# Low halves of the down projections' weights: an adding DMA onto negated high halves in place of a VectorE subtraction

## The chip, the cores and the metric

The kernel runs on one core of a Trainium2 chip. The metric is device time in microseconds, from the first to the last instruction of one execution and the little that lies around them, median over the executions. The engines have short names here: PE is the tensor engine, DVE the vector engine, ACT the scalar engine, POOL is GpSimd, SP the sync engine, which in this kernel issues nearly all transfers. A name with a q behind it (SPq) is an engine's queue of instructions that are not compute.

## The reference

One decoder layer on 256 positions with 2048 channels, all in float32: a half-step SwiGLU feed-forward (hidden size 5632), a mixer of a state-space group and a gated MLP group, a second feed-forward, and a gated embedding. Only the feed-forwards matter for the change:

```python
def swiglu(x, w_gate, w_up, w_down):
    return (jax.nn.silu(x @ w_gate) * (x @ w_up)) @ w_down
...
    h = h + 0.5 * swiglu(rms_norm(h, norm_ffn1[i]), w1_gate[i], w1_up[i], w1_down[i])
...
    h = h + 0.5 * swiglu(rms_norm(h, norm_ffn2[i]), w2_gate[i], w2_up[i], w2_down[i])
```

## The kernel before

**Three products for one.** Every large product is done in the tensor engine's rounded float32 format, with both operands split in two: a high half (the value rounded to that format) and a low half (the value less its high half). For each weight `w` there are `wh` and `wl`, for each activation a high and a low one, and `products` issues three matmuls for each tile: activation high by `wh`, activation high by `wl`, activation low by `wh`. They add up in one PSUM accumulator (`acc`).

**Units.** A Group is a product with 512 output columns (`n0`), over `kt` tiles of 128 rows of the weight. A load takes four of these tiles (128 x 2048 float32, 1 MB) into one of three `raw` buffers. A pair (`KS = 2` tiles, half a load) is the unit of the splitting and of the products: its `wh` and `wl` are tiles of 128 x 1024, each from a pool of four buffers, and it feeds 12 matmuls (2 tiles x 2 halves of the positions x 3). The down projections are `w1_down` and `w2_down`: 4 groups of 44 tiles each, so 22 pairs in a group and 88 pairs in each of the two.

**Order.** The kernel's order is written out by hand in `stream`. For pair i on PE it first calls `do_split` up to pair i + 3, then issues the products of pair i. `do_split` issues loads two ahead on SP, then ACT's copy of `raw` to `wh` (line 133), then DVE's subtraction `wl = raw - wh` (line 134). Since `wh` and `wl` have four buffers, the split of pair i + 3 can begin when the products of pair i - 1 are done, and is needed when the products of pair i + 2 are done. A load's buffer comes free when ACT and DVE have read it. At the end of a down group `down_post` adds the accumulators to `h` (DVE, line 390), squares (ACT, line 223), and transposes `h` on PE, with splits on ACT and DVE (lines 214 and 217).

In the down projections the activations are `gTa` and `gTb`, so the matmuls of these stages can be told by their names `gTah`, `gTal`, `gTbh`, `gTbl`. GpSimd has no DMA of its own in this kernel.

Of the kernel before, what the change touches and what calls it, by code (L numbers as in the profile page):

```python
# [7 lines left out]
F32 = mybir.dt.float32  # L8
F32R = mybir.dt.float32r
I32 = mybir.dt.int32  # L10
AF = mybir.ActivationFunctionType
ALU = mybir.AluOpType
# [9 lines left out]
NW = 512  # L22
KL = 4
# [25 lines left out]
class Group:  # L49
    def __init__(self, w, n0, kt, act, post, kbase=0):  # L50
        self.w, self.n0, self.kt, self.act, self.post, self.kbase = w, n0, kt, act, post, kbase
        self.ps = None


class Layer:
# [9 lines left out]
        self.queue.append([self.tick_no + delay, gen])  # L65

    def paced(self, gen):
        """emits what gen emits, at most about self.budget us of VectorE time in a tick; gen yields
        the time of what it emitted (a float) or the ticks to wait (an int)"""
        acc = 0.0  # L70
        for c in gen:
            if isinstance(c, int):
                yield c
                acc = 0.0
            else:
                acc += c
                if acc >= self.budget:
                    yield 1
                    acc = 0.0
# [14 lines left out]
    def stream(self):  # L94
        nc = self.nc
        subs, loads = [], []
        for g, k0, nk in self.plan:
            li = len(loads)
            loads.append((g, k0, nk))
            for s0 in range(0, nk, KS):  # L100
                subs.append((g, li, s0, k0 + s0, min(KS, nk - s0)))
        n = len(subs)
        tail = self.plan[-1][0]
        n_tail = sum(sb[0] is tail for sb in subs)
        raws, split = {}, {}
        state = {"ld": 0, "sp": 0}

        def load(li):
            for f in self.preload.pop(li, ()):
                f()  # L110
            g, k0, nk = loads[li]
            t = self.raw_p.tile([P, KL, NW], F32, tag="raw", name="raw")
            kq, kr = divmod(g.kbase + k0, KL)
            nc.sync.dma_start(out=t[:, 0:nk, :], in_=g.w[g.n0 // NW, kq, :, kr:kr + nk, :])
            raws[li] = t

        def do_split():
            i = state["sp"]
            state["sp"] += 1
            g, li, s0, k0, nk = subs[i]  # L120
            while state["ld"] <= min(li + 2, len(loads) - 1):
                load(state["ld"])
                state["ld"] += 1
            for f in self.presplit.pop(i, ()):
                f()
            src = raws[li][:, s0:s0 + nk, :]
            if g is tail and i < n - LA_SPLIT - 1:
                wh = self.pools["tail"].tile([P, KS, NW], F32R, tag=f"wh{i}", name="wht")
                wl = self.pools["tail"].tile([P, KS, NW], F32R, tag=f"wl{i}", name="wlt")
            else:  # L130
                wh = self.wh_p.tile([P, KS, NW], F32R, tag="wh", name="wh")
                wl = self.wl_p.tile([P, KS, NW], F32R, tag="wl", name="wl")
            nc.scalar.activation(out=wh[:, 0:nk, :], in_=src, func=AF.Copy)  # L133
            nc.vector.tensor_tensor(  # L134
                out=wl[:, 0:nk, :], in0=src, in1=wh[:, 0:nk, :].bitcast(F32), op=ALU.subtract)
            split[i] = (wh, wl)

        def products(i, ts, ps=None, c0=0, c1=NW):
            g, li, s0, k0, nk = subs[i]
            wh, wl = split[i]  # L140
            for j in range(nk):
                k = k0 + j
                for t in ts:
                    ah, al = g.act(k, t)
                    first, last = k == 0, k == g.kt - 1
                    o = (ps or g.ps[t])[:, c0:c1]
                    nc.tensor.matmul(o, ah, wh[:, j, c0:c1], start=first, stop=False)  # L147
                    nc.tensor.matmul(o, ah, wl[:, j, c0:c1], start=False, stop=False)  # L148
                    nc.tensor.matmul(o, al, wh[:, j, c0:c1], start=False, stop=last)  # L149

        for i in range(n):
            ahead = i + LA_SPLIT + 1
            if i > n - 2 * n_tail:
                ahead += (i - (n - 2 * n_tail)) // 2
            while state["sp"] < min(ahead, n):
                do_split()
            g, li, s0, k0, nk = subs[i]
            if k0 == 0:
                g.ps = [self.acc_p.tile([P, NW], F32, tag="acc", name=f"acc{t}") for t in range(2)]
            if g is tail:  # L160
                products(i, (0,))
            else:
                products(i, range(2))
                split.pop(i)
            if k0 + nk == g.kt:
                self.spawn(g.post(g, 0, 0) if g is tail else g.post(g))
            self.tick_no += 1
            self.run_due()
        late = self.acc_p.tile([P, NW], F32, tag="acc", name="late")
        for part, ps in enumerate((tail.ps[1], late)):  # L170
            for i in range(n - n_tail, n):
                products(i, (1,), ps, part * NW // 2, (part + 1) * NW // 2)
                self.tick_no += 1
                if i == n - 1:
                    tail.ps[1] = ps
                    self.spawn(tail.post(tail, 1, part))
                self.run_due()
        while self.queue:
            self.tick_no += 1
            self.run_due()  # L180
# [28 lines left out]
            out=dl, in0=src, scalar=g, in1=dh.bitcast(F32), op0=ALU.mult, op1=ALU.subtract)  # L209

    def split_gain2(self, ps, g, dh, dl):
        """two k tiles that lie in one bank; g, dh, dl start at the first of them"""
        for kk in range(2):
            self.nc.scalar.activation(out=dh[:, kk, :], in_=ps[:, kk * 256:kk * 256 + 256], func=AF.Copy,
                                      scale=g[:, kk:kk + 1])
        for kk in range(2):
            self.nc.vector.scalar_tensor_tensor(
                out=dl[:, kk, :], in0=ps[:, kk * 256:kk * 256 + 256], scalar=g[:, kk:kk + 1],
                in1=dh[:, kk, :].bitcast(F32), op0=ALU.mult, op1=ALU.subtract)
# [3 lines left out]
        self.nc.scalar.activation(out=j, in_=src, func=AF.Square, accum_out=acc)  # L223

    def h_to_T(self, n, gcol):
        """transposes of chunk n of h, gain applied, into hT"""
        for b in range(2):
            yield 1
            k0 = 4 * n + 2 * b
            ps = self.transposes(  # L230
                [self.h[:, t, (k0 + kk) * P:(k0 + kk + 1) * P] for kk in range(2) for t in range(2)])
            self.split_gain2(ps, self.gcol[:, gcol + k0:gcol + k0 + 2], self.hTh[:, k0:k0 + 2], self.hTl[:, k0:k0 + 2])
# [4 lines left out]
    def kernel(self):  # L237
        tc, nc, I = self.tc, self.nc, self.i
# [27 lines left out]
        self.ffn_groups(2)  # L266
        self.ple_groups()

        # products that nothing reads keep the tensor engine's clock up until the first weights are here
        warm = self.aux_p.tile([P, NW], F32, tag="aux", name="warm")  # L270
        for _ in range(N_WARM):
            nc.tensor.matmul(warm[:, 0:P], self.ident, self.ident, start=True, stop=True)
# [48 lines left out]
        self.pools.pop(key)  # L321
        self.cms.pop(key).__exit__(None, None, None)

# [1 line left out]
    KA = 24  # L325

    def open_g(self):
# [15 lines left out]
    def ffn_groups(self, which):  # L343
        I = self.i
        wg, wu, wd = (I[f"w{which}_{n}"] for n in ("gate", "up", "down"))
# [59 lines left out]
                self.whole(gate)  # L405
            self.whole(Group(wu, c * NW, 16, self.act_hT, up_post(c)))
        for n in range(4):
            self.whole(Group(wd, n * NW, 44, act_g, down_post(n)))

# [1 line left out]
    def vexp(self, pool, x, out):  # L411
        """out = exp(x) for [128, 32] tiles, relative error of a few 2^-24"""
        v = self.nc.vector
        t = {n: pool.tile([P, 32], F32, tag=f"ex{n}", name=f"ex{n}") for n in "xnra"}
        v.tensor_scalar(out=t["x"], in0=x, scalar1=-88.0, scalar2=88.5, op0=ALU.max, op1=ALU.min)
# [15 lines left out]
    def s5_tables(self):  # L431
        nc, I, g, v = self.nc, self.i, self.nc.gpsimd, self.nc.vector
# [25 lines left out]
        are, aim, ldt = (prm[:, i, :] for i in range(3))  # L458
# [74 lines left out]
        for k in range(NQ):  # L533
# [6 lines left out]
            u1, u2, bbr, bbi = (T(n, (P, 8, 16)) for n in ("u1", "u2", "bbr", "bbi"))  # L540

            def cmul(xr_, xi_, yr, yi, outs_r, outs_i, neg=False):
                """(xr_ + i xi_)(yr + i yi); the imaginary part negated on demand"""
                gop(u1, yr, xr_, M)
                gop(u2, yi, xi_, M)
                yield 0.4
# [18 lines left out]
            for i in range(2):  # L565
                s = slice(64 * i, 64 * i + 64)
# [20 lines left out]
            for q in range(8):  # L587
                o = ps[64 * (q % 2):64 * (q % 2) + 64, 32 * (q // 2):32 * (q // 2) + 32]
                for ri in range(2):
                    nc.tensor.matmul(o, ea[ri][:, q].rearrange("p t g x -> p (t g x)"),  # L590
                                     cp[ri][:, q].rearrange("p g x -> p (g x)"),
                                     start=(ri == 0), stop=(ri == 1))
# [4 lines left out]
            for a in range(2):  # L597
                s = slice(64 * a, 64 * a + 64)
# [22 lines left out]
                    yield cost  # L621
            put(k, 0, 2, 512)

# [1 line left out]
    def close_mix(self):  # L625
        for n in ("yss", "mix", "qt"):
            self.close(n)
# [29 lines left out]
        self.nc.sync.dma_start(out=self.qt[b], in_=self.stash[b])  # L657

    def s5_block(self, n):
        """four pairs of groups: 2 * 64 states and 2 * 32 channels each"""  # L660
        nc, g, v = self.nc, self.nc.gpsimd, self.nc.vector
        m = self.pools["mix"]
        qt = self.qt[n]
# [4 lines left out]
        u = m.tile([P, 256], F32, tag=f"u{par}", name="u")  # L668
        nc.scalar.activation(out=u, in_=ps[:, 0:256], func=AF.Copy)
        yield 1  # L670
        # one bank for each half of the rows of the tensor engine
        vb = [self.aux_p.tile([P, NW], F32, tag="aux", name=f"v{x}") for x in range(2)]
        for ri in range(2):
            for i in range(4):
# [246 lines left out]
        for n in range(4):  # L921
            G(Group(wo, n * NW, 8, act_ss, wo_post(n, self.r[5], True)))

# [1 line left out]
    def ple_groups(self):  # L925
        I, nc = self.i, self.nc
        r = self.r[4]
# [165 lines left out]
```

## Time and profile before

| | |
|---|---|
| device time, median of 2 runs (lowest to highest) | 1886.81 us (1885.71 to 1887.91) |
| profiled execution, span | 1884.0 us |
| PE busy | 1868.6 us (99%) |
| DVE busy | 1118.2 us (59%) |
| ACT busy | 842.7 us (45%) |
| POOL busy | 57.5 us (3%) |
| moved by DMA | 373.64 MB, 198 GB/s on average |

The page says how long each engine was busy and what moved. The timeline gives single instructions with the idle time of their engine before them. The windows give sums for a stretch, with the granted clock (1.00 is TensorE's higher level, 2.4 GHz, and 0.50 the lower, 1.2 GHz) and the mean busy share of the 16 DMA engines.

### The profile page before, as it was taken

What the parts mean: (1) busy time and instruction counts of PE and PEld (TensorE: products, weight loads), DVE (VectorE), ACT (ScalarE), POOL (GpSimd) and SP (SyncE); (2) the same over time, 40 slices, a digit from 0 to 9 for tenths busy, and PEclk for the clock granted to TensorE, in tenths of its full rate; (3) what the DMA queues carried; (4) which work ended last, traced back from release to release, by engine and by line L of the source; (5) the groups of instructions that cost most, each with busy time, mean ns of one, the idle gap of its engine ahead of it and who ended that gap; (6) DMA issues with size and microseconds to landing.
All of it is one profiled execution on the core that took longest, in us unless ns stands there. A gap on an engine that the chain in (4) does not pass through costs nothing.

```text
span 1884.0 us, 21981 instructions
## 1 busy us (share of the span) xinstructions
PE 1868.6 (99%) x8752; PEld 1551.3 (82%) x8752; DVE 1118.2 (59%) x1516; ACT 842.7 (45%) x1014; POOL 57.5 (3%) x60
## 2 busy tenths in 40 slices
PE   9999999999999999999999999999999999999998
PEld 7888888888888888887888888888888888888887
DVE  6788886455445554688876545455544444455565
ACT  6444444444444444434446544444444444344454
POOL 1000000000000000033100000000000000000000
PEclk9999999999999999999999999999999999999999
DMA  8556665554555555665545555555555555555553
GB/s 330 197 208 237 237 228 222 182 198 178 189 193 198 182 196 182 230 240 199 189 161 179 201 181 199 180 197 182 183 197 187 193 184 196 190 190 188 198 201 134
DMA packets 62534, 373.64 MB, mean 198 GB/s; under 512 B 7776, under 2 KB 13152, under 8 KB 19808
## 3 DMA queue, kind: packets, MB, share of 16 engines
q1 hardware_dynamic: 62000, 371.67, 54.7%
q8 instruction: 68, 1.11, 0.2%
q10 hardware_dynamic: 432, 0.57, 0.1%
q14 instruction: 34, 0.28, 0.0%
HBM read 360.55 MB, written 11.53 MB: 197 GB/s over the span
## 4 chain that ended last, share of the span: by engine, by line
PE 53%; DVE 0%; POOL 0%; issue 0%; ACT 0%; POOLq 0%; DVEq 0%; ACTq 0%
PE acc L147 17%; PE acc L149 17%; PE acc L148 17%; PE tr L199 1%; PE sp L766 0%; PE y L725 0%; POOL gv L843 0%; PE v L678 0%; DVE tf L701 0%; PE y L719 0%; PE late L149 0%; PE late L148 0%; PE late L147 0%; DVE gv L841 0%; DVE tb L701 0%
## 5 line engine op out<-in xcount | busy, mean ns | idle before, releaser
L134 DVE TENSOR_TENSOR wl<-raw,wh 128x1024 fp32r<-128x1024 f32 (+1 forms) x649 | 801.9, 1237 | 661.1 <-ACT wh L133 657.8
L133 ACT ACTIVATE wh<-raw 128x1024 fp32r<-128x1024 f32 (+1 forms) x649 | 686.2, 1058 | 773.3 <-PE acc L149 745.1
L147 PE MATMUL acc<-wh,hTh 128*128 128x512 f32 (+1 forms) x1744 | 684.8, 393 | 0.2 <-ACT wh L133 0.2
L148 PE MATMUL acc<-wl,hTh 128*128 128x512 f32 (+1 forms) x1744 | 678.5, 389 | 0.8 <-DVE wl L134 0.8
L149 PE MATMUL acc<-wh,hTl 128*128 128x512 f32 (+1 forms) x1744 | 679.1, 389 | 0.0
L149 PEld LDWEIGHTS acc<-wh,hTl 128*128 128x128 f32 x1744 | 327.4, 188 | 68.6
L148 PEld LDWEIGHTS acc<-wl,hTh 128*128 128x128 f32 x1744 | 327.7, 188 | 67.9 <-DVE wl L134 1.8
L147 PEld LDWEIGHTS acc<-wh,hTh 128*128 128x128 f32 x1744 | 327.6, 188 | 66.9 <-ACT wh L133 0.6
L147 PE MATMUL acc<-wh,gTah 128*128 128x512 f32 x384 | 150.9, 393 | 0.0
L149 PE MATMUL acc<-wh,gTal 128*128 128x512 f32 x384 | 149.7, 390 | 0.0
L148 PE MATMUL acc<-wl,gTah 128*128 128x512 f32 x384 | 149.5, 389 | 0.0
L148 PE MATMUL acc<-wl,gTbh 128*128 128x512 f32 x320 | 124.5, 389 | 0.0
L149 PE MATMUL acc<-wh,gTbl 128*128 128x512 f32 x320 | 124.5, 389 | 0.0
L147 PE MATMUL acc<-wh,gTbh 128*128 128x512 f32 x320 | 124.5, 389 | 0.0
L149 PEld LDWEIGHTS acc<-wh,gTal 128*128 128x128 f32 x384 | 72.1, 188 | 15.2
L148 PEld LDWEIGHTS acc<-wl,gTah 128*128 128x128 f32 x384 | 72.2, 188 | 14.6
L147 PEld LDWEIGHTS acc<-wh,gTah 128*128 128x128 f32 x384 | 72.1, 188 | 14.5
L149 PEld LDWEIGHTS acc<-wh,gTbl 128*128 128x128 f32 x320 | 60.1, 188 | 12.5
L147 PEld LDWEIGHTS acc<-wh,gTbh 128*128 128x128 f32 x320 | 60.1, 188 | 12.5
L148 PEld LDWEIGHTS acc<-wl,gTbh 128*128 128x128 f32 x320 | 60.1, 188 | 12.4
L194 POOL TENSOR_TENSOR r<-rs,mhalf 128x2 f32<-128x2 f32 x6 | 5.1, 856 | 1354.6 <-DVE rs L193 1343.8
L360 ACT ACTIVATE g<-acc,r 128x512 f32<-128x512 f32 x44 | 29.9, 689 | 19.8 <-PE acc L149 19.8
(227 smaller groups left out, 1065.7 us busy)
## 6 DMA issues: line engine op xcount, KB each, us to landing
raw<-in_w_up SPq DMA_DIRECT2D x88, 1024.0 KB, 4.8
raw<-in_w_down SPq DMA_DIRECT2D x88, 1024.0 KB, 4.8
raw<-in_w_gate SPq DMA_DIRECT2D x86, 1024.0 KB, 4.8
raw<-in_w_in SPq DMA_DIRECT2D x24, 1024.0 KB, 4.9
raw<-in_w_out SPq DMA_DIRECT2D x16, 1024.0 KB, 4.8
raw<-in_w_ple_gate SPq DMA_DIRECT2D x16, 1024.0 KB, 4.8
qt<-stash SPq DMA_DIRECT2D x8, 1152.0 KB, 5.2
stash<-qt SPq DMA_DIRECT2D x8, 640.0 KB, 4.5
```

The source lines that it names most:

```text
L133: nc.scalar.activation(out=wh[:, 0:nk, :], in_=src, func=AF.Copy)
L134: nc.vector.tensor_tensor(out=wl[:, 0:nk, :], in0=src, in1=wh[:, 0:nk, :].bitcast(F32), op=ALU.subtract)
L147: nc.tensor.matmul(o, ah, wh[:, j, c0:c1], start=first, stop=False)
L148: nc.tensor.matmul(o, ah, wl[:, j, c0:c1], start=False, stop=False)
L149: nc.tensor.matmul(o, al, wh[:, j, c0:c1], start=False, stop=last)
L194: nc.gpsimd.tensor_tensor(out=out, in0=s2, in1=self.mhalf, op=ALU.pow)
L199: self.nc.tensor.transpose(ps[:, i * P:(i + 1) * P], b, self.ident)
L360: self.nc.scalar.activation(out=st[c][t], in_=g.ps[t], func=AF.Silu, scale=r[:, t:t + 1])
```

## The change

In the groups of the down projections, a pair with an index that `lo_dma` divides gets its `wl` in another way. ACT copies `wh` into `wl` with the sign turned, and a DMA issued by GpSimd then reads the weights of the pair from HBM once more and adds them to what stands in `wl`: `wl = -wh + w`. In the first down projection this is every second pair (44 of 88), in the second every pair (88). The other pairs, and all other products, keep the subtraction on DVE. The other hunks of the diff only take out comments.

```diff
@@ class Group
         self.ps = None
+        self.lo_dma = 0
...
@@ Layer.stream, do_split
             nc.scalar.activation(out=wh[:, 0:nk, :], in_=src, func=AF.Copy)
+            if g.lo_dma and i % g.lo_dma == 0:
+
+                nc.scalar.activation(out=wl[:, 0:nk, :], in_=wh[:, 0:nk, :].bitcast(F32), func=AF.Copy, scale=-1.0)
+                kq, kr = divmod(g.kbase + k0, KL)
+                nc.gpsimd.dma_start(out=wl[:, 0:nk, :], in_=g.w[g.n0 // NW, kq, :, kr:kr + nk, :], accum_op=ALU.add)
+                split[i] = (wh, wl)
+                return
             nc.vector.tensor_tensor(
                 out=wl[:, 0:nk, :], in0=src, in1=wh[:, 0:nk, :].bitcast(F32), op=ALU.subtract)
             split[i] = (wh, wl)
...
@@ Layer.ffn_groups
         for n in range(4):
-            self.whole(Group(wd, n * NW, 44, act_g, down_post(n)))
+            g = Group(wd, n * NW, 44, act_g, down_post(n))
+            g.lo_dma = 2 if which == 1 else 1
+            self.whole(g)
```

ACT's instructions where the first down projection begins (line 133 before and 134 after are the copy to `wh`, 203 and 211 belong to the activations); the number behind a name is that of its buffer. Before:

```order
L133 ACTIVATE wh_4060<-raw_3990 128x1024
L133 ACTIVATE wh_4076<-raw_3990 128x1024
L133 ACTIVATE wh_4094<-raw_4024 128x1024
L133 ACTIVATE wh_4112<-raw_4024 128x1024
L203 ACTIVATE gTbh_2924<-tr_4130 128x512
```

and with the change:

```order
L134 ACTIVATE wh_4060<-raw_3990 128x1024
L134 ACTIVATE wh_4076<-raw_3990 128x1024
L137 ACTIVATE wl_4077<-wh_4076 128x1024
L134 ACTIVATE wh_4095<-raw_4024 128x1024
L134 ACTIVATE wh_4113<-raw_4024 128x1024
L137 ACTIVATE wl_4114<-wh_4113 128x1024
L211 ACTIVATE gTbh_2924<-tr_4132 128x512
```

The new copy stands behind the `wh` of the second half of each load, so the added transfer of a load comes right after the point where its `raw` buffer is given back.

GpSimd's queue at the same place, with the change (616 and 617 belong to tables set up long before; 139 is the adding DMA); before, the same queue had no DMA here:

```order
L616 MEMSET qt_352 128x8
L617 MEMSET qt_352 128x8
L139 DMA wl_4077<-in_w1_down 128x1024
L139 DMA wl_4114<-in_w1_down 128x1024
L139 DMA wl_4165<-in_w1_down 128x1024
```

The second down projection on ACT, with the change:

```order
L134 ACTIVATE wh_11472<-raw_11363 128x1024
L137 ACTIVATE wl_11473<-wh_11472 128x1024
L134 ACTIVATE wh_11491<-raw_11399 128x1024
L137 ACTIVATE wl_11492<-wh_11491 128x1024
L134 ACTIVATE wh_11508<-raw_11399 128x1024
L137 ACTIVATE wl_11509<-wh_11508 128x1024
```

Here every copy to `wh` is followed by its negation, two instructions for a pair where there was one.

## Rows read from the trace of the kernel before

**Rows 1.** The page: span, and busy time, share and instructions of each engine
```profile
span 1884.0 us, 21981 instructions
PE 1868.6 (99%) x8752; PEld 1551.3 (82%) x8752; DVE 1118.2 (59%) x1516; ACT 842.7 (45%) x1014; POOL 57.5 (3%) x60
```

**Rows 2.** Waits of PE over the whole span: waiting line <- releaser: us, times, longest
```profile
PE sp L766 <- POOL gv L843: 4.4, 1, 4.4
PE warm L272 <- POOL mhalf L251: 1.4, 1, 1.4
PE acc L148 <- DVE wl L134: 0.8, 1, 0.8
PE acc L147 <- ACT wh L133: 0.2, 1, 0.2
```

**Rows 3.** Second down product, timeline: start us, us, engine line op [idle before <-releaser]
```profile
1621.11 0.39 PE L149 MATMUL acc<-wh,gTal 128*128 128x512 f32 x1
1621.34 0.39 PE L147 MATMUL acc<-wh,gTah 128*128 128x512 f32 x1
1621.54 1.06 ACT L133 ACTIVATE wh<-raw 128x1024 fp32r<-128x1024 f32 x1 [1.66 <-PE acc L149]
1621.57 0.39 PE L148 MATMUL acc<-wl,gTah 128*128 128x512 f32 x1
1622.63 1.23 DVE L134 TENSOR_TENSOR wl<-raw,wh 128x1024 fp32r<-128x1024 f32 x1 [1.49 <-ACT wh L133]
1623.88 5.77 SPq L114 DMA_DIRECT2D raw<-in_w_down  x2
1624.26 1.06 ACT L133 ACTIVATE wh<-raw 128x1024 fp32r<-128x1024 f32 x1 [1.66 <-PE acc L149]
1629.72 0.39 PE L148 MATMUL acc<-wl,gTbh 128*128 128x512 f32 x1
```

**Rows 4.** Windows (length; busy PE, PEld, DVE, ACT, POOL; clock; DMA share; GB/s): downs, start-up
```profile
560.00:614.40 54.40, 54.40 (x245) 45.03 (x244) 27.41 (x26) 23.12 (x28) 0.00 (x0) 1.00 0.53 192
1620.00:1674.40 54.40, 54.40 (x245) 45.06 (x244) 27.38 (x26) 23.16 (x28) 0.00 (x0) 1.00 0.52 191
10.00:35.00 25.00, 24.23 (x105) 19.31 (x105) 16.66 (x23) 19.04 (x35) 3.87 (x6) 1.00 1.01 406
```

**Rows 5.** DMA of 15 to 35 us: all packets, and one queue issue row
```profile
DMA packets 1601, 8.33 MB, mean 417 GB/s; under 512 B 432, under 2 KB 432, under 8 KB 688
raw<-in_w_up SPq DMA_DIRECT2D x4, 1024.0 KB, 9.1
```

**Rows 6.** The page: DMA issues, KB each, median us from issue to landing
```profile
raw<-in_w_down SPq DMA_DIRECT2D x88, 1024.0 KB, 4.8
raw<-in_w_ple_proj SPq DMA_DIRECT2D x4, 512.0 KB, 3.7
```

**Rows 7.** ACT in the timeline at the end of a second-down group
```profile
1590.64 1.06 ACT L133 ACTIVATE wh<-raw 128x1024 fp32r<-128x1024 f32 x1 [1.66 <-PE acc L149]
...
1594.98 1.04 ACT L133 ACTIVATE wh<-raw 128x1024 fp32r<-128x1024 f32 x1
...
1597.25 1.06 ACT L133 ACTIVATE wh<-raw 128x1024 fp32r<-128x1024 f32 x1
...
1600.46 1.06 ACT L133 ACTIVATE wh<-raw 128x1024 fp32r<-128x1024 f32 x1
```

**Rows 8.** Windows as in group 4: around a wait of PE, and at the start
```profile
880.00:882.00 2.00, 0.00 (x0) 0.00 (x0) 1.97 (x3) 0.14 (x1) 2.00 (x1) 0.98 0.91 385
884.00:886.00 2.00, 2.00 (x11) 2.00 (x11) 1.97 (x4) 0.00 (x0) 0.00 (x0) 0.50 0.00 0
890.00:892.00 2.00, 2.00 (x12) 1.63 (x11) 2.00 (x7) 0.00 (x0) 1.49 (x2) 1.00 0.88 340
10.00:12.00 2.00, 1.23 (x5) 0.86 (x5) 1.73 (x3) 0.91 (x3) 0.00 (x0) 1.00 0.95 322
```

**Rows 9.** By tile: durations ns min/median/max of SP's issue and of GpSimd's longest operation
```profile
L114 SPq DMA_DIRECT2D raw<-in_w_down x88: 327/328/328, 487.4 to 1751.0; - x88
L843 POOL TENSOR_TENSOR gv<-gv,gvb x2: 2396/3693/4990, 872.0 to 878.6; 128x1024 f32<-128x1024 f32 x2
```

## The prediction

> **What bounds the kernel now.** I read the page's busy times first: PE is busy 1868.6 of 1884.0 us, DVE 59%, ACT 45% [rows 1]. The list of PE's waits comes next. Four waits, 6.8 us in all, are the whole of what PE waited for during 1884 us; only one of 0.8 us is for DVE's subtraction, and none stands in a down projection [rows 2]. The windows over the two down projections say the same for the stages that are changed: PE 54.40 of 54.40 us at a granted clock of 1.00, DVE 27.4, ACT 23.1, POOL 0, and the 16 DMA engines 0.52 to 0.53 busy at 191 to 192 GB/s [rows 4]. So in these stages TensorE is the bound and everything else has room. DVE's work, which the change takes away, costs nothing there now.
>
> The timeline shows how much room. ACT begins a `wh` every 2.72 us (1621.54 and 1624.26), the period of one pair of 12 matmuls. The copy begins just after the last matmul that reads the old content of that buffer (start 1621.11, 0.39 us) has ended, takes 1.06 us, and DVE's subtraction follows at 1622.63 and takes 1.23 us, to 1623.86. The first matmul that reads this `wl` is that of three pairs later: 1621.57 + 3 x 2.72 = 1629.73, which is the row at 1629.72. So `wl` now lies finished for 5.9 us before it is wanted [rows 3].
>
> **What the change removes.** In 132 of 176 pairs DVE loses a subtraction of 1.23 us. With no wait of PE on it in these stages, the gain is 0. The most that any change off PE could bring in the whole kernel is 1884.0 - 1868.6 = 15.4 us, and that lies in waits and in the start and the tail elsewhere [rows 1, 2].
>
> **What it adds on ACT.** One copy of 128 x 1024 for each such pair. A negating copy does not occur in this trace; the nearest row is the copy to `wh`, same engine, size and function, 1.06 us [rows 3]. In the second down projection ACT then works 2 x 1.06 = 2.12 us of each 2.72, and at a group's end the squares and splits delay it: `wh` at 1594.98 is 1.7 us late against 1590.64 + 2.72, the next two 1.2 and 1.7 us [rows 7]. ACT still fits; what it costs is the start of the transfer behind it.
>
> **The new deadline.** The chain of a pair becomes copy, negation, GpSimd's issue, transfer. From ACT's start 1621.54 the negation ends at about 1621.54 + 2 x 1.06 = 1623.7. The deadline stays at 1629.7. So from the end of the negation to the landing there are L = 6.0 us. If the landing comes x later, PE stands still, and since a buffer comes back every fourth pair, it stands x once in four pairs: 22 times in each of the two stages. Behind GpSimd's waiting DMA only further adding DMAs are queued, and no other engine wants GpSimd there.
>
> **What the adding transfer costs.** There is no adding DMA and no DMA issued by GpSimd in the trace, so I bound both. From below: it costs what a plain 512 KB load costs, 3.7 us to landing [rows 6], and its issue SP's 0.33 us [rows 9]. Then L holds, and the load of the DMA engines goes from 1 MB to 2 MB for each two pairs. From above: it costs three passes over 512 KB (read the weights, read `wl`, write `wl`, each like a plain load), and GpSimd's issue takes as long as its longest operation here, 3.7 us [rows 9]. Between them I take two passes: a plain load reads 512 KB, this one reads 1 MB, the weights and the old `wl`. The nearest row is then the plain 1 MB load with 4.8 us to landing [rows 6].
>
> For what the DMA engines can carry I read the start-up, the only stretch where they are full: 417 GB/s in 15 to 35 us, at a share of 1.01 over 10 to 35 us, and 1 MB loads land after 9.1 us there [rows 4, 5]. So 1 MB (1.049 million bytes) is 2.51 us of all 16 engines. Two pairs last 2 x 2.72 = 5.44 us.
>
> Second down projection: 1 MB plain and two adding transfers of two passes are 3 MB, 3 x 2.51 = 7.54 us against 5.44 (with r passes 2.51 x (1 + r)). The DMA engines become the bound, 2.10 us late for each two pairs, 44 times: +92 us. With the share as measured in these stages in place of the rate (0.52 x 5.44 = 2.83 us for 1 MB [rows 4]) it is 8.49 us, +134 us.
>
> First down projection: one adding transfer for two pairs, 2 MB, 5.03 us of 5.44. This fits, but with little room, and the added transfer begins about when the plain load does, which SP issues when the second `wh` of its buffer is made, 1.1 us ahead of the end of the negation. Of the plain load's 2.51 us up to 1.4 can lie ahead of it: 4.8 + 1.4 = 6.2 us, and with half a microsecond for GpSimd's slower start (my choice; no row has it) 6.7, 0.7 over L. 22 x 0.7 = +15 us; by the bounds 0 (3.7 us) and 22 x 3.1 = +68 us (9.1 us). ACT's delay at the ends of the 4 groups, 1.7 us each, adds 7 us. In the second stage it hides behind the full DMA engines.
>
> There is a rule of the Trainium skill on an adding DMA, and it speaks against the change: in "Collectives: The Full Stack", section "The bandwidth ceiling: the fold count and why AG ≠ RS ≠ AR", a reduce step runs at about half a copy's rate, because it reads two sources on one read ring. By it the second stage is bound as in the sum above; with the plain 512 KB row alone there would be no such bound. No run here shows it yet.
>
> **Sum.** 0 (DVE) + 92 + 15 + 7 = +114 us. The profiled span is 1884.0 us, 2.8 below the median of the runs, 1886.8; on that median: 2001 us.
>
> **Rivals.**
>
> *Hidden.* The added read of `wl` is free beside the read from HBM: one pass. Then two pairs of the second stage need 5.03 us of 5.44 and the landing keeps L. Price 0, time 1887; with small misses up to 1915. For it: 0.47 of the DMA engines is idle in these stages [rows 4], and a 512 KB load lands in 3.7 us. Against it: 92% of what the engines ever carried would have to go without queueing. It decides at (5.44 - 2.51) / 2.51 = 1.17 passes: above that the second stage cannot hold 2.72 us. Its sign is the other one: not slower. Nothing makes the kernel faster by 2% (38 us), since only 15.4 us are idle on PE.
>
> *Late, not full.* One pass, but a long way: GpSimd's issue or the completion takes long, and each landing comes up to 9.1 us after the negation, as in the start-up. 22 x 3.1 = 68 us in each stage, +136 at most, 1930 to 2020. It would show in both stages alike, where my forecast shows almost all in the second.
>
> *Three passes, or a slow GpSimd.* Second stage: 2.51 + 2 x 3.77 = 10.06 us for two pairs, +4.62 x 44 = 203; first: 6.28, +0.84 x 44 = 37; together +240, 2127 us. A GpSimd that needs 3.7 us for one issue would bound the second stage alone: 0.98 x 88 = +86, inside my range.
>
> *The clock falls.* PE's one long wait in the trace (4.4 us) was followed by a granted clock of 0.50, the 1.2 GHz level, in 884 to 886, and it was 1.00 again by 890; a window at the start in which PE stood still for 0.77 of 2 us kept 1.00 [rows 2, 8]. My stalls are 1 to 2 us for each pair or two. If they too bring the clock down in half of the second stage, a pair there takes 5.44 instead of 3.77 us: 44 x 1.67 = +73 on top, 2074.
>
> **How the numbers follow.** Two passes with full DMA engines: 0.50, of its own range 1960 to 2075 (below: 1.8 passes, 2.51 x 2.8 = 7.03 us for two pairs, +70, and nothing in the first stage; above: the 134 us, or the clock). Hidden: 0.24. Late, not full: 0.08. Three passes and more: 0.17. Faster: 0.01. The prediction is the likeliest, 2001 us. A range that leaves out 2 in 10 reaches down to the hidden case and gives up the three passes: 1886 to 2075. By 2%, about what a measurement of this kernel can tell from no change (38 us): faster 0.01, same 0.24, slower 0.75.
>
> **What would show it.** In the windows of the second down projection: DMA share near 1.0, PE busy near 5.44 / 7.54 = 0.72, the stage about 330 us in place of 240. PE's waits should name the DMA of `wl` at the matmul on `wl`, some 90 us in the second stage, 10 to 25 in the first. The landing of the adding DMA: above 6 us in both, near 7 in the first, 8 to 10 in the second. ACT should have no wait for DVE there. The prediction is wrong if the DMA share of the second stage stays well below 1 while PE waits (then it is the way, not the load), if the first stage loses as much as the second, or if PE does not wait at all.

## The result and the profile after

The changed kernel takes 2036.29 us (median of 2 runs, 2032.15 to 2040.43) against 1886.81: a ratio of 1.079, 95% interval 1.077 to 1.081, so 149.5 us slower. The forecast was 2001 us, in a range of 1886 to 2075. The sign was right, and so was what holds the second stage, which lost the most; the loss of the first stage was put at less than half of what it was.

The page of the changed kernel, span and busy times, which answer to [rows 1]:

```profile
span 2030.5 us, 22257 instructions
PE 1906.5 (94%) x8752; PEld 1549.8 (76%) x8752; DVE 958.5 (47%) x1384; ACT 981.0 (48%) x1146; POOL 169.0 (8%) x192
```

DVE fell by 160 us and ACT rose by 138, as the change says; the span rose by 146.5. PE's "busy" rose by 38 us although its matmuls are the same 8752. PE's waits answer to [rows 2] (us in total, times, longest):

```profile
PE acc L156 <- DMA wl<-in_w_down: 107.7, 84, 3.0
PE sp L776 <- POOL gv L853: 4.4, 1, 4.4
PE acc L156 <- DVE wl L142: 1.4, 2, 0.8
```

One line is new: PE waits 107.7 us for the DMA into `wl`, in 84 waits. By stage, the first down projection and then the second, these are

```profile
PE acc L156 <- DMA wl<-in_w_down: 37.7, 36, 2.2
PE acc L156 <- DMA wl<-in_w_down: 69.9, 48, 3.0
```

How long each stage lasts is seen from the first and the last matmul of each down projection, by the tile. Of the kernel before (columns: durations ns min/median/max, first and last start us):

```profile
L147 PE MATMUL acc<-wh,gTah x192: 387/389/477, 506.0 to 721.4; 128*128 128x512 f32 x192
L147 PE MATMUL acc<-wh,gTbh x160: 389/389/390, 539.6 to 748.6; 128*128 128x512 f32 x160
L147 PE MATMUL acc<-wh,gTah x192: 387/389/477, 1532.4 to 1747.7; 128*128 128x512 f32 x192
L147 PE MATMUL acc<-wh,gTbh x160: 389/389/390, 1566.0 to 1774.9; 128*128 128x512 f32 x160
```

And of the changed one:

```profile
L155 PE MATMUL acc<-wh,gTah x192: 387/389/476, 506.5 to 767.0; 128*128 128x512 f32 x192
L155 PE MATMUL acc<-wh,gTbh x160: 387/389/397, 548.8 to 799.1; 128*128 128x512 f32 x160
L155 PE MATMUL acc<-wh,gTah x192: 387/389/632, 1582.1 to 1882.4; 128*128 128x512 f32 x192
L155 PE MATMUL acc<-wh,gTbh x160: 387/389/632, 1630.0 to 1921.3; 128*128 128x512 f32 x160
```

The first stage lasted 748.6 - 506.0 = 242.6 us and now 799.1 - 506.5 = 292.6: **+50.0**. The second lasted 1774.9 - 1532.4 = 242.5 and now 1921.3 - 1582.1 = 339.2: **+96.7**. The sum, 146.7, is the whole difference of the spans (146.5). The same two differences are used for every experiment below.

What filled up is in the windows (columns as in [rows 4]), first stage and second:

```profile
620.00:720.00 100.00, 88.30 (x376) 68.23 (x375) 22.73 (x22) 51.31 (x54) 13.80 (x16) 1.00 0.92 243
1582.00:1921.00 339.00, 268.73 (x1086) 202.25 (x1085) 14.73 (x25) 192.17 (x199) 75.04 (x86) 0.97 1.04 274
```

The DMA engines went from 0.52 to 1.04 in the second stage and to 0.92 in the first, and PE fell from all of the time to 79% and 88%. The queues in 100 us of the second stage (q0 is GpSimd's queue with the adding DMAs, q1 SP's with the plain loads; packets, MB, share of the 16 engines) price the transfers:

```profile
q0 software_dynamic: 3690, 13.41, 69.2%
q1 hardware_dynamic: 1840, 13.49, 34.4%
raw<-in_w_down SPq DMA_DIRECT2D x13, 1024.0 KB, 9.1
wl<-in_w_down POOLq DMA_DIRECT2D x26, 512.0 KB, 9.8
```

q0 moved 13.41 / 0.524 = 25.6 transfers of 512 KB in 69.2 us of all engines, 2.70 us each. q1 moved 13.49 / 1.049 = 12.9 loads of 1 MB in 34.4 us, 2.67 us each. **An adding DMA of 512 KB occupies the engines as long as a plain load of 1 MB**, which is what two passes were to cost. It is the time that shows this, not the bytes: the whole page counts 69.21 MB on q0, which is 132 x 0.524, each added byte once. Both kinds of transfer now land after more than 9 us, against 4.8 us of a load before [rows 6].

The timeline of the second stage shows one stall, rows left out between them (start us, us, engine line op, idle before and its releaser):

```profile
1741.77 1.06 ACT L137 ACTIVATE wl<-wh 128x1024 fp32r<-128x1024 f32 x1
1743.12 0.87 POOL L139 DMA_DIRECT2D wl<-in_w_down  x1 [3.83 <-ACT wl L137]
1745.67 0.50 PE L156 MATMUL acc<-wl,gTbh 128*128 128x512 f32 x1 [2.01 <-DMA wl<-in_w_down]
1746.47 0.52 PE L156 MATMUL acc<-wl,gTbh 128*128 128x512 f32 x1
1747.64 0.63 PE L156 MATMUL acc<-wl,gTbh 128*128 128x512 f32 x1
1748.92 0.63 PE L156 MATMUL acc<-wl,gTbh 128*128 128x512 f32 x1
1750.12 0.39 PE L156 MATMUL acc<-wl,gTbh 128*128 128x512 f32 x1
1750.81 0.39 PE L156 MATMUL acc<-wl,gTbh 128*128 128x512 f32 x1
```

ACT's negation ends at 1742.83, GpSimd begins 0.29 us later and takes 0.87 us to issue. PE has stood for 2.01 us when an earlier `wl` is there. After it matmuls on `wl`, three matmuls apart, follow each other after 0.80, 1.17, 1.28 and 1.20 us where 0.68 is normal, which the last section comes back to.

### The profile page after: what moved, and what is told of

Its sections match the earlier page's. It is cut to its first block, busy times and chain, and to the rows that moved or that the text cites. A ratio compares the mean times of both kernels' runs of the same rounds, so it can differ in the third digit from the quotient of the medians.

```text
span 2030.5 us, 22257 instructions
## 1 busy us (share of the span) xinstructions
PE 1906.5 (94%) x8752; PEld 1549.8 (76%) x8752; DVE 958.5 (47%) x1384; ACT 981.0 (48%) x1146; POOL 169.0 (8%) x192
## 3 DMA queue, kind: packets, MB, share of 16 engines
q0 software_dynamic: 19008, 69.21, 18.0%
HBM read 429.76 MB, written 11.53 MB: 217 GB/s over the span
## 4 chain that ended last, share of the span: by engine, by line
PE 41%; DMA 12%; issue 1%; DVE 0%; POOL 0%; ACT 0%; POOLq 0%; DVEq 0%; ACTq 0%
PE acc L156 13%; PE acc L157 13%; PE acc L155 13%; DMA wl<-in_w_down 12%; PE tr L207 1%; PE sp L776 0%; PE y L735 0%; POOL gv L853 0%; DVE tf L711 0%; PE v L688 0%; PE y L729 0%; DVE gv L851 0%; POOL wl L139 0%; DVE tb L711 0%; DVE hg L1025 0%
## 5 line engine op out<-in xcount | busy, mean ns | idle before, releaser
L142 DVE TENSOR_TENSOR wl<-raw,wh 128x1024 fp32r<-128x1024 f32 (+1 forms) x517 | 640.8, 1241 | 693.8 <-ACT wh L134 691.1
L139 POOL DMA_DIRECT2D wl<-in_w_down x132 | 115.0, 871 | 1238.4 <-ACT wl L137 1164.3
L156 PE MATMUL acc<-wl,gTah 128*128 128x512 f32 x384 | 158.7, 413 | 55.3 <-DMA wl<-in_w_down 54.9
L156 PE MATMUL acc<-wl,gTbh 128*128 128x512 f32 x320 | 130.9, 409 | 52.7 <-DMA wl<-in_w_down 52.7
L137 ACT ACTIVATE wl<-wh 128x1024 fp32r<-128x1024 f32 x132 | 139.9, 1060 | 4.2
L398 DVE SCALAR_TENSOR_TENSOR h<-acc,h 128x512 f32<-128x512 f32 x16 | 10.9, 690 | 225.6 <-PE acc L157 225.6
```

Of the source, the lines that this page charges most:

```text
L137: nc.scalar.activation(out=wl[:, 0:nk, :], in_=wh[:, 0:nk, :].bitcast(F32), func=AF.Copy, scale=-1.0)
L139: nc.gpsimd.dma_start(out=wl[:, 0:nk, :], in_=g.w[g.n0 // NW, kq, :, kr:kr + nk, :], accum_op=ALU.add)
L142: nc.vector.tensor_tensor(out=wl[:, 0:nk, :], in0=src, in1=wh[:, 0:nk, :].bitcast(F32), op=ALU.subtract)
L398: self.nc.vector.scalar_tensor_tensor(out=hs, in0=g.ps[t], scalar=0.5, in1=hs, op0=ALU.mult, op1=ALU.add)
```

## The experiments

Each row of this table is the gain or loss of a stage against the 242.6 and 242.5 us of before, from the same four rows of its trace, and the median landing of the transfers into `wl` in the two stages. Lead stands for one more `wl` buffer and an earlier start, as told below.

| kernel | us (ratio, 95%) | first stage | second stage | landing, us |
|---|---|---|---|---|
| the change | 2036.3 (1.079, 1.077 to 1.081) | +50.0 | +96.7 | 7.6, 9.7 |
| plain in place of adding DMA | 1941.5 (1.029, 1.027 to 1.031) | +14.5 | +40.4 | 5.5, 6.6 |
| negation alone, no DMA | 1885.8 (0.9996, 0.9987 to 1.0006) | 0 | 0 | none |
| negation first | 2022.5 (1.072, 1.070 to 1.074) | +45.0 | +92.5 | 8.3, 11.0 |
| one pair more of lead | 1985.4 (1.053, 1.050 to 1.055) | +12.7 | +88.2 | 8.2, 13.2 |
| the other half of the pairs in the first stage | 2024.3 (1.073, 1.070 to 1.076) | +37.7 | +99.5 | 7.4, 9.7 |
| lead and plain DMA | 1888.8 (1.0013, 1.0002 to 1.0025) | 0 | +1.0 | 5.4, 7.0 |
| every fourth pair in both | 1948.1 (1.033, 1.030 to 1.036) | +33.0 | +28.7 | 6.7, 6.5 |
| source in SBUF | 2043.0 (1.083, 1.080 to 1.086) | +45.2 | +109.0 | 5.5, 8.8 |
| lead, every second pair in both | 1906.6 (1.011, 1.009 to 1.013) | +9.0 | +11.1 | 8.3, 8.4 |
| lead, every fourth pair in both | 1885.8 (0.9998, 0.9989 to 1.0008) | 0 | 0 | 5.6, 5.6 |

**What the addition costs.** The transfer stays, the addition goes:

```diff
-                nc.gpsimd.dma_start(out=wl[:, 0:nk, :], in_=g.w[g.n0 // NW, kq, :, kr:kr + nk, :], accum_op=ALU.add)
+                nc.gpsimd.dma_start(out=wl[:, 0:nk, :], in_=g.w[g.n0 // NW, kq, :, kr:kr + nk, :])
```

> The change with the addition taken out of the DMA: GpSimd's transfers stay in place and size, but write the weights plainly over the negated copy (so wl holds w instead of w less wh). Theory (an adding transfer is two passes of the DMA engines, 2.66 us of all 16 for 512 KB as in the trace after, against 2.65 us for a plain 1 MB load): here it falls to about 1.33 us, two pairs of the second stage need 2.65 + 2 x 1.33 = 5.3 of 5.44 us, its share stays below 1.0, and the stage loses 0 to 40 us for lateness in place of 97; the first loses 0 to 20 in place of 50; 1890 to 1945 us in all. Rival (GpSimd's way of issuing is what is slow, whatever the DMA does): landings stay at 7.6 and 9.7 us, time near 2036.

1941.5 us. The rival falls: the same transfers without the addition give 55 of the 147 us. The first stage lost 14.5 (0 to 20 expected), the second 40.4, just above the 0 to 40 expected; which of lateness and load that 40 is, the trace of this run alone didn't say (DMA share 0.96 in 1700 to 1800).

**What ACT's second copy costs.** The copy stays, the transfer goes:

```diff
-                kq, kr = divmod(g.kbase + k0, KL)
-                nc.gpsimd.dma_start(out=wl[:, 0:nk, :], in_=g.w[g.n0 // NW, kq, :, kr:kr + nk, :], accum_op=ALU.add)
```

> Only ACT's half of the change: the negated copy stays, the adding DMA is left out (wl holds minus wh). Theory (ACT's second copy of 1.06 us per pair fits in 2.72 us and costs nothing by itself): 1884 to 1892 us, no wait of PE in the down projections. Rival (ACT at over 80% in the second stage is late at the ends of the groups and holds PE up): 4 x 1.7 us per stage and more, 1895 to 1910.

1885.8 us. ACT is busy 183.94 of 230 us in the second stage and PE all of it:

```profile
1540.00:1770.00 230.00, 230.00 (x1028) 190.42 (x1027) 10.59 (x19) 183.94 (x191) 0.00 (x0) 1.00 0.53 192
```

So neither the second copy nor the lighter DVE (10.59 us) changes anything. The prediction had put 7 us on ACT's delays at the ends of the groups, through the start of the transfer behind them. This run has no such transfer, so it shows only that the delays cost nothing by themselves.

**An earlier start by 1.06 us.** ACT negates `raw` first, then copies it to `wh`:

```diff
-            nc.scalar.activation(out=wh[:, 0:nk, :], in_=src, func=AF.Copy)
             if g.lo_dma and i % g.lo_dma == 0:
-                nc.scalar.activation(out=wl[:, 0:nk, :], in_=wh[:, 0:nk, :].bitcast(F32), func=AF.Copy, scale=-1.0)
+                nc.scalar.activation(out=wl[:, 0:nk, :], in_=src, func=AF.Copy, scale=-1.0)
...
+                nc.scalar.activation(out=wh[:, 0:nk, :], in_=src, func=AF.Copy)
                 split[i] = (wh, wl)
                 return
+            nc.scalar.activation(out=wh[:, 0:nk, :], in_=src, func=AF.Copy)
```

> The change with ACT's two copies in the other order: the negated copy is made from raw, ahead of the copy to wh, so each adding DMA starts 1.06 us sooner; nothing else differs. Theory (the first stage loses by lateness, once in each ring of four pairs, while the second is held by full DMA engines): the first stage gains 22 x 1.06 = 23 us, the second nothing; 2010 to 2018 us. Rival 1 (the first stage too is held by full DMA engines): 2030 to 2040. Rival 2 (both stages are held by lateness): twice the gain, 1988 to 1996.

2022.5 us, between theory (2010 to 2018) and rival 1 (2030 to 2040): a miss. The first stage gained 5 us, not 23. The landing grew from 7.6 to 8.3 us and took most of the start back. The two transfers now begin nearer to each other (near 640 us they are issued 0.7 us apart in place of 1.4), and the engines at 0.92 have little room. That this is why the landing grew was not tried by itself.

**One pair more of lead.** A fifth `wl` buffer, and the negation (made from `raw`) and the DMA of pair i + 1 are issued behind the `wh` of pair i:

```diff
+        def lo_pre(i):
+            g, li, s0, k0, nk = subs[i]
+            if not g.lo_dma or i % g.lo_dma or i in pre:
+                return
+            wl = pre[i] = self.wl_p.tile([P, KS, NW], F32R, tag="wl", name="wl")
+            nc.scalar.activation(out=wl[:, 0:nk, :], in_=raws[li][:, s0:s0 + nk, :], func=AF.Copy, scale=-1.0)
+            kq, kr = divmod(g.kbase + k0, KL)
+            nc.gpsimd.dma_start(out=wl[:, 0:nk, :], in_=g.w[g.n0 // NW, kq, :, kr:kr + nk, :], accum_op=ALU.add)
...
             nc.scalar.activation(out=wh[:, 0:nk, :], in_=src, func=AF.Copy)
+            if i + 1 < n:
+                lo_pre(i + 1)
...
-                pool(name="wl", bufs=LA_SPLIT + 1)
+                pool(name="wl", bufs=LA_SPLIT + 2)
```

> The change with a fifth wl buffer: the negated copy is made from raw, and it and the adding DMA are issued one pair earlier than the split of that pair, so a landing has about 2.7 + 1.1 us more. Traffic is the same. Theory (lateness in the first stage, full DMA engines in the second): the first stage loses at most 15 us in place of 50, the second still 85 to 100; 1975 to 2000 us. Rival 1 (full engines in both stages): near 2036. Rival 2 (lateness in both stages): both vanish, 1887 to 1920.

1985.4 us, as the theory said and unlike both rivals. The same traffic with 3.8 us more room takes 37 of the 50 us from the first stage and 8.5 of the 97 from the second:

```profile
1546.00:1877.00 331.00, 261.27 (x1089) 194.90 (x1088) 15.27 (x25) 182.03 (x198) 74.15 (x85) 1.00 1.05 280
507.00:763.00 256.00, 246.54 (x1089) 200.47 (x1089) 66.90 (x69) 142.55 (x156) 37.16 (x43) 1.00 0.97 271
```

The first stage was held by lateness, the second by full engines (1.05 with the lead, 1.04 without).

**The other half of the load.** In the first stage the adding DMA serves the first half of a load:

```diff
-            if g.lo_dma and i % g.lo_dma == 0:
+            if g.lo_dma and i % g.lo_dma == g.lo_dma - 1:
```

> The change with the other half of the pairs in the first stage: the first half of each load in place of the second, so that the adding DMA no longer starts within 1.3 us of SP's plain load but half a period away from it. The second stage is the same. Theory (in the first stage the landing of 7.6 us is the adding transfer's own 5.7 to 6.5 us and the rest is the collision with the plain load): the median landing falls to 6.0 to 6.8 us, the first stage loses 5 to 30 us in place of 50, time 1990 to 2018 us. Rival (the landing is the adding transfer's own): 7.3 us or more, 2030 to 2040 us.

2024.3 us, 6 above the theory's range, and the landing 7.4, between theory and rival: another miss for the collision as I had pictured it. The first stage loses 12 us less, but now SP's loads land after 7.4 us in place of 5.5 (both in 620 to 720 us). With the engines at 0.91 of the time there may be no place in the period where one transfer doesn't meet the other; that is how I read it, and no run sets it apart.

**Lead and no addition.** In the kernel with the lead:

```diff
-            nc.gpsimd.dma_start(out=wl[:, 0:nk, :], in_=g.w[g.n0 // NW, kq, :, kr:kr + nk, :], accum_op=ALU.add)
+            nc.gpsimd.dma_start(out=wl[:, 0:nk, :], in_=g.w[g.n0 // NW, kq, :, kr:kr + nk, :])
```

> The kernel with a fifth wl buffer and one pair more of lead, with the addition taken out of its DMA (plain transfers over the negated copy, wl holds w in place of w less wh). Theory (what the plain transfers still lost without the lead, 14 and 40 us, was lateness: landings of 5.5 and 6.6 us plus GpSimd's issue against 6.0): both fall to 0 to 15 us, 1887 to 1910 us. Rival (the engines at a share of 0.96 are full for one pass too): the second stage keeps 30 us or more, 1917 to 1945 us.

1888.8 us: the second stage loses 1 us, the first nothing. So the 40 us of the plain transfers were lateness. PE's waits, and the queues of the second stage:

```profile
PE acc L165 <- DMA wl<-in_w_down: 0.3, 1, 0.3
```

```profile
q0 software_dynamic: 5186, 18.88, 52.7%
q1 hardware_dynamic: 2567, 18.67, 49.6%
```

Here the engines carry the weights twice, 18.88 + 18.67 MB in 100 us, and everything is hidden. Their share is 1.02 (52.7 and 49.6%), hardly below the 1.04 of the change. So a share near 1 does not by itself show that the engines hold PE; what shows it is the time that comes back when each transfer takes less of them. A plain 512 KB transfer by GpSimd takes 52.7 / 36 = 1.46 us of all engines, the adding one 2.70. Against the kernel with the lead, which differs by the addition alone, the second stage loses 87 us less. **These 87 us come with the addition alone, for the same bytes on the same queues.** Whether it is the reading of the old `wl` or the adding that takes the time, no run tells.

**A quarter.** Every fourth pair in both stages:

```diff
-            g.lo_dma = 2 if which == 1 else 1
+            g.lo_dma = 4
```

> The change with every fourth pair in both stages: 22 adding DMAs in each, all in the same wl buffer. Two passes: 2.51 x 1.5 = 3.8 us of 5.44 for two pairs, so the engines are not full. Theory (lateness counts once in each ring of four pairs, however few of them are by DMA): landings of 5.7 to 6.8 us and 0.3 us ahead of GpSimd's issue against 6.0 lose 0 to 1.1 us in each of 22 rings, 0 to 25 us a stage, 1887 to 1935 us. Rival (loss goes with the number of adding DMAs, a quarter of the 97 us of the second stage in each): 2 x 24 = +48, 1930 to 1940 us.

1948.1 us, 13 above the theory's range, and above the rival's too. The waits of PE in the two stages:

```profile
PE acc L156 <- DMA wl<-in_w_down: 23.4, 21, 2.5
```

```profile
PE acc L156 <- DMA wl<-in_w_down: 20.7, 20, 2.2
```

One wait for nearly each of the 22 rings (of four `wl` buffers), 1.1 us long. A landing of 6.6 us and 0.3 us ahead of the issue is 0.9 over the 6.0 us; the rest of the 1.3 to 1.5 us that each wait costs lies in what follows it (below). Half as many adding DMAs as in the first stage of the change lose two thirds of what those lose, and by itself that lies between the theory and the rival. The waits speak for the theory. In the first stage of the change a landing is 7.6 + 0.3 - 6.0 = 1.9 us late, and PE waits 37.7 / 22 = 1.7 us for each ring, spread over 36 waits: the second late transfer of a ring is late only by what the first wait has not already covered. Clearest are the plain transfers without lead, whose 88 transfers of the second stage make 24 waits:

```profile
PE acc L156 <- DMA wl<-in_w_down: 26.6, 24, 2.1
```

**The source in SBUF.** The adding DMA reads the `raw` buffer:

```diff
-                nc.gpsimd.dma_start(out=wl[:, 0:nk, :], in_=g.w[g.n0 // NW, kq, :, kr:kr + nk, :], accum_op=ALU.add)
+                nc.gpsimd.dma_start(out=wl[:, 0:nk, :], in_=src, accum_op=ALU.add)
```

> The change with the adding DMA's source in SBUF: it adds the pair's half of the raw buffer in place of reading the weights from HBM again, so HBM is read once as before. A raw buffer comes back only when the adds that read it have landed, which may make plain loads late. Theory (an adding transfer is two passes of the DMA engines wherever its source lies): some 2.6 us of all engines for each as in the change, the second stage loses 90 us or more, 2025 to 2100 us. Rival (the second read of HBM is what fills up): under 2 us for each, the second stage loses under 50 us, below 1990.

2043.0 us. HBM is read once (360.55 MB in the whole execution as before, against 429.76 with the change), and the second stage still loses 109 us. In 1640 to 1740 us the queue of the adding DMAs takes

```profile
q0 software_dynamic: 3454, 12.57, 64.5%
wl<-raw POOLq DMA_DIRECT2D x25, 512.0 KB, 9.1
```

64.5 / (12.57 / 0.524) = 2.69 us for each: the same price without a second read of HBM. It is this price that speaks here, and not the loss of the stages, which may have a second cause: a `raw` buffer is free for SP's next load only when the adds that read it have landed, and ACT now waits for the loads into `raw`, 20.4 us in 490 to 800 us and 105.7 in 1500 to 1935, where in the change it waited for none. The first stage loses 45.2 us though its adding transfers land after 5.5. How much of either loss the late loads make up wasn't tried by itself.

**Same dose in both stages.** The kernel with the lead, and in it:

```diff
-            g.lo_dma = 2 if which == 1 else 1
+            g.lo_dma = 2
```

> The kernel with a fifth wl buffer and one pair more of lead, with every second pair by the adding DMA in both stages. Theory (the second stage loses by the number of passes, not by anything else that sets it apart from the first): with the same dose both stages lose the same 8 to 18 us, 1903 to 1922 us. Rival (something of the second projection itself, its weights in HBM or the work around it, costs part of the 88 us): the second stage loses over 30 us, above 1930.

1906.6 us, +9.0 and +11.1: the two projections behave alike at the same dose, the share of the pairs that go by an adding DMA. So it was for its dose that the second lost more than the first in the change.

**A dose that is hidden.** The same with

```diff
-            g.lo_dma = 2 if which == 1 else 1
+            g.lo_dma = 4
```

> The same with every fourth pair in both stages: 44 adding DMAs, 3.8 to 4.2 us of the 16 engines in 5.44 us, and about 9.8 us of room for a landing of some 6.6. Theory: everything is hidden, PE waits for no wl, and since the subtraction on DVE was hidden too, the time is that of before, 1884 to 1891 us. Rival (each adding DMA costs PE something even when it lands in time, such as slower matmuls while it reads and writes SBUF): 0.3 us or more for each, 1900 us and above. Rival 2 (a lighter DVE does give time back): below 1880.

1885.8 us. Landings of 5.6 us, PE without a wait for any DMA:

```profile
PE sp L785 <- POOL gv L862: 3.9, 1, 3.9
PE warm L289 <- POOL mhalf L268: 1.4, 1, 1.4
PE acc L165 <- DVE wl L151: 0.8, 1, 0.8
```

```profile
510.00:740.00 230.00, 230.00 (x1029) 190.41 (x1028) 87.47 (x83) 117.89 (x131) 18.11 (x21) 1.00 0.78 239
1540.00:1770.00 230.00, 230.00 (x1027) 190.43 (x1026) 86.37 (x82) 116.97 (x129) 18.28 (x21) 1.00 0.78 236
```

DVE has 87 us of work in 230 where it had 27.38 of 54.40 [rows 4], that is 116 of 230, and nothing comes of it. Both rivals fall: at this dose an adding DMA that lands in time costs PE nothing, and a lighter DVE gives nothing back.

## Why the prediction was right, and where its sum was off

**What bounds the kernel** held. PE was the bound in the down projections, and taking work from DVE gained nothing: shown by the negation alone (0.9996) and the hidden dose (0.9998).

**The second stage: +92 forecast, +96.7 measured.** The step that carried it was the choice of two passes, between one and three. No row of the trace of before stood behind it, and the prediction gave it 0.50: that it came out is partly luck. It measured 2.70 us for 512 KB against 2.67 us for a plain 1 MB, and 2.69 us with the source in SBUF. The rate came out as read from the start-up: 3 MB for two pairs in 339.2 / 44 = 7.71 us, and 330.7 / 44 = 7.52 with the lead, forecast 7.54. So the full engines alone cost 88.2 us, near the 92, and the other 8.5 went with the lead: lateness or the clock, for which the sum had no term in this stage. Of the chain of evidence, taking the addition away from the kernel with the lead (-87 us) is the shortest. The rule of the Trainium skill that was weighed there ("Collectives: The Full Stack", section "The bandwidth ceiling: the fold count and why AG ≠ RS ≠ AR") is stated of the reduce step of a collective, which runs at about half a copy's rate for its two reads. The traces agree with its size for a DMA that adds into SBUF, from HBM or from SBUF: 2.70 / 1.33 = 2.0 against half of the 1 MB load, 1.85 against GpSimd's own plain transfer. That two reads are the reason, no run here shows.

**The first stage: +22 forecast (15 and 7), +50.0 measured.** The mechanism, lateness that counts once in a ring of four pairs, was right: the lead took 37 us of it away, and the waits per ring follow the landing (1.7 us where it is 1.9 late, 1.1 where it is 1.0). The term that was mis-sized is the 0.7 us by which the landing was to come after L. I took 4.8 us for the transfer alone, as for a plain 1 MB load, 1.4 for the collision and 0.5 for GpSimd: 6.7. Measured, a landing is 5.6 to 6.6 us where the engines are at 0.72 to 0.78 (hidden dose, quarter), in the stage 7.6, and GpSimd starts 0.3 us after the negation: 7.9 from its end, 1.9 over the 6.0. 22 x 1.9 = 42 us, of which PE's waits show 37.7. The other 12.3 of the 50.0 us stand in PE's busy time, which rose from 242.6 to 255.3 us in the stage: each wait costs more than its length (last section), for which the sum had no term. Nor does a run show the 7 us for ACT at the ends of the groups; the delays cost nothing by themselves.

**The collision** with the plain load was pictured too simply. Two runs that moved the adding DMA in time (1.06 us sooner, half a period away) gained 5 and 12 us where 23 and 20 to 45 were expected. At 0.91 to 0.92 of the engines' time the transfers may share wherever they stand; what makes the landing 7.6 us and not 6.6 stays open.

**The rivals.** *Hidden* would have needed at most 1.17 passes, and the plain transfers with lead show that one pass does fit. *Late, not full* is what the first stage was, and not the second. *Three passes* fell with the 2.70 us. *The clock falls* was partly there: the mean granted clock of the second stage was 0.97; with the lead it was 1.00 and the loss still 88.2 us. So what clock and lateness add to the full engines is 8.5 us of the 96.7, not the 73 that I had set as a price for the clock.

**What was to show it** did: DMA share 1.04, PE at 0.79 (0.72 forecast), the stage 339 us (330), landings of 7.6 and 9.7 us (7, and 8 to 10). PE's waits named the DMA but gave only 69.9 us in the second stage (90 forecast), and 37.7 in the first (10 to 25); the rest is in slower matmuls and starts, which the page counts as busy. The range from 1886 to 2075 us held everything from no change to two passes and a slow clock, so that 2036 lies in it says little; the two stages, the share and the landings say more.

## What to carry to other kernels

An engine that is half busy beside a full TensorE, and that TensorE does not wait for, was no place to gain. A transfer that replaces its work must be counted in the time it takes of the DMA engines: here an adding DMA of 512 KB into SBUF counted twice its bytes, with its source in HBM or in SBUF. Before a step is moved to a DMA, work out both its load (share of the engines over one period) and its way (landing against the lead that the buffers give). The two need different cures: one more buffer took 37 of 50 us from the first stage, where the way was the trouble, and 8.5 of 97 from the second, where the load was; there only less work for the engines helped (no addition, or fewer adding DMAs).

## What the runs showed of the hardware that I had not expected

A wait of PE costs more than its length. Part of that is in the counting: in the stream the matmuls start 0.23 us apart and each is listed with 0.39 [rows 3], so the last one before a wait counts some 0.16 us that it would have shared with the next. Part of it is a slow start. In the timeline above, after a wait of 2.01 us, the matmuls first come 0.80 us apart by threes, then 1.17 to 1.28, and 0.69 only from 1750.12 on. The granted clock of the same stretch:

```profile
1740.00:1742.00 2.00, 2.00 (x10) 1.53 (x9) 0.00 (x0) 1.29 (x2) 0.00 (x0) 1.00 1.01 272
1744.00:1746.00 2.00, 0.33 (x1) 0.30 (x2) 0.00 (x0) 1.58 (x2) 0.09 (x1) 1.00 1.03 270
1746.00:1748.00 2.00, 2.00 (x7) 1.59 (x6) 0.00 (x0) 0.00 (x0) 0.79 (x1) 0.65 1.06 209
1748.00:1750.00 2.00, 2.00 (x6) 1.56 (x5) 0.00 (x0) 0.00 (x0) 0.00 (x0) 0.50 1.06 328
1750.00:1752.00 2.00, 2.00 (x10) 1.64 (x10) 0.00 (x0) 1.95 (x2) 0.00 (x0) 1.00 1.02 317
```

PE was busy 0.33 of 2 us in 1744 to 1746, and the granted clock was 0.65, then 0.50 (1.2 GHz) in the 4 us after that, and 1.00 in the next window. So a wait of 2 us was followed by the lower level, where before only one of 4.4 us had shown it [rows 8]. Not each such wait was: after those of 2.48 us (at 1805.36) and 2.01 us (at 1862.95) in the same stage the windows stay at 1.00, as they do in the kernel with the lead, whose longest is 2.3 us. What sets them apart, the runs do not show. After a wait of 0.56 us, in the first stage, only the first step of three matmuls is longer (0.80, then 0.69):

```profile
645.75 0.50 PE L156 MATMUL acc<-wl,gTbh 128*128 128x512 f32 x1 [0.56 <-DMA wl<-in_w_down]
646.55 0.40 PE L156 MATMUL acc<-wl,gTbh 128*128 128x512 f32 x1
647.24 0.40 PE L156 MATMUL acc<-wl,gTbh 128*128 128x512 f32 x1
```

By these rows a wait at full clock costs 0.16 + 0.11 us on top of its length. For the 36 waits of the first stage that is some 10 of the 12.3 us that it lost beside them, by my estimate.

The issue of an adding DMA keeps GpSimd for 0.87 us, that of the same transfer without the addition for 0.53 us (medians 872 and 527 to 540 ns), both above the 0.33 us of SP's issue [rows 9].
